# Sorting a recurrence's small matmuls by shape: within-chunk products first, state products after, and block scores in one written-out order

## The chip, the cores and the metric

The kernel runs on one core of one Trainium2 chip. The metric is the device time of one execution, in microseconds (us), lower is better. A core has a matmul engine (TensorE, PE in the profile; its weight loads are shown apart as PEld), three engines for vectors and scalars (VectorE or DVE, ScalarE or ACT, GpSimd or POOL) and a queue that issues most of the DMA transfers (SyncE or SP). Each engine works through its own list of instructions in order, and the engines wait for each other by semaphores.

## The reference, cut to what matters

One layer of a diffusion trunk over 640 tokens (128 of a prompt, 512 latent ones) of width 1024: an input projection, three groups of heads that read it (A: differential attention, B: a bidirectional gated linear recurrence, C: grouped-query attention), an output projection, and a squared-ReLU MLP. The change is in group B, which has four heads with a 64x64 state in each direction, scanned in chunks of 64 tokens:

```python
def step(S, xs):                       # one chunk of one direction
    qc, kc, vc, gc = xs
    b = jnp.cumsum(gc, axis=1)
    o_inter = jnp.einsum('bthk,bhkv->bthv', qc * jnp.exp(b), S)            # state product
    ...
    attn = jnp.einsum('bthk,bshk,btshk->bths', qc, kc, decay)              # scores in the chunk
    o_intra = jnp.einsum('bths,bshv->bthv', attn, vc)                      # within-chunk product
    S = jnp.exp(b_end)[..., None] * S + jnp.einsum('bshk,bshv->bhkv', kc * jnp.exp(b_end[:, None] - b), vc)
    return S, o_inter + o_intra
```

## The kernel before

Everything is float32. Large products (projections, MLP) split both operands in a high and a low part and take three matmuls for each product; these have a stationary operand of 128x128 and are called the GEMMs below. The small products of group B are plain float32 matmuls. The profile records each float32 matmul as two instructions, so that a count in the profile is twice the count in the program.

Group B works head by head (h = 0 to 3). Both directions are stacked on the 128 partitions, rows 0 to 63 forward and 64 to 127 backward. The 640 tokens are 10 chunks of 64, in 5 pairs of 128 tokens, and the pairs are taken in two groups, of 2 and 3 pairs.

- `b_scores(h)` makes the scores `att`, group by group. The score matrix of a chunk can't be made by one matmul, because the decay between two tokens is a ratio of exponentials that would overflow. It is built from levels: for L = 32, 16 and 8, VectorE and ScalarE write scaled keys and queries `lk[L]`, `lq[L]` (the tile `b_lqk`), and `blocks` multiplies them block by block. Level 32 has blocks of 64 and starts the accumulation in `pl`; level 16 has blocks of 32 and adds to `pl`; level 8 has blocks of 64 into `p8`. All these contract over 128 rows. Then come the two 64-row products of the tiles `k8` and `q8` (forward rows `F`, backward rows `R`) into the PSUM tile `ps2`, and the undecayed product of keys and queries into `pd`. `pl`, `p8` and `pd` lie in one PSUM tile, `pslv` in the profile; `ps2` is `psl`. ScalarE copies `pl` to `att`, and VectorE overwrites the entries that the four masks name from `p8`, from both halves of `ps2` and from `pd` (COPY_PREDICATED).
- `b_state(h)` makes the state updates (`psu`), VectorE scans them chunk by chunk into `st`.
- `b_out(h)` makes the output in the PSUM tile `psob`: for each of the 10 chunks the within-chunk product (64 rows of `att` with 64 rows of the values, rows and output partitions alternating between the halves) and then the state product (`qhat` with `st`, 128 rows), which adds to it.

A scheduler decides the order in each engine's list; it lets GEMMs and the adaLN products (`psada`) of other steps stand between the small matmuls. A `tc.manual_schedule` block keeps the matmuls in it in the order in which they are written, though other steps can still come between them. The calls at the end set the rough order: the scores of heads 0 to 3, the GEMMs `psgb` (gate) and `psA` (group A), and the adaLN columns lie around each other, then attention, output projection and MLP. PSUM tiles of the tag `s`, which `pslv`, `psl`, `psu` and `psob` share, have two buffers. Weights come through two raw buffers (`wr`) and are split by ScalarE and VectorE into five pairs of `wh` and `wl`, which the adaLN weights (`wad`) also use.

Of the kernel before, what the change touches and what calls it, by code (L numbers as in the profile page):

```python
# [28 lines left out]
HD = 64  # L29
# [13 lines left out]
CH = 64  # L43
NCH = NTOK // CH
# [19 lines left out]
def hybrid_layer_kernel(ctx: ExitStack, tc: tile.TileContext, T):  # L64
    nc = tc.nc
    V, A, G, PE = nc.vector, nc.scalar, nc.gpsimd, nc.tensor
# [96 lines left out]
    ib = mixed[:, 0:2, :].rearrange("p a (b c) -> p (a b c)", c=P).rearrange("p (t v) -> p t v", v=256)  # L163
# [6 lines left out]
    with ExitStack() as sctx:  # L170
# [66 lines left out]
        with tc.manual_schedule(engines={mybir.EngineType.PE}):  # L237
            for j in range(NK):
# [21 lines left out]
                r = sp.tile([P, 2 * P], F32, tag="adar", name=f"adar{j}", bufs=2)  # L260
# [26 lines left out]
    def ps_o(name):  # L287
        return pps.tile([P, 512], F32, tag="o", name=name, bufs=2)

    def ps_s(name):  # L290
        return pps.tile([P, 1024], F32, tag="s", name=name, bufs=2)

    def p1t(tag, shape, dtype=F32, bufs=1, name=None):
        return p1.tile(shape, dtype, tag=tag, name=name or tag, bufs=bufs)
# [134 lines left out]
    lq, lk = {}, {}  # L429
# [5 lines left out]
    def mrep(i, n):  # L435
        return masks[:, i : i + 1, :].to_broadcast([P, n, CH])

    F, R = slice(0, HD), slice(HD, P)
# [9 lines left out]
    def b_scores(h):  # L448
        k, b = bk[h], bb[h]
        hc = slice(h * HD, (h + 1) * HD)  # L450
        q = p1t(("a_kd0", "u6")[h % 2], [P, NTOK], name=f"b_q2{h}")
        src = bq[h // 2][(h % 2) * HD : (h % 2 + 1) * HD, :]
        A.copy(q[F], src)
        A.copy(q[R], src)
        att = p1t(("a_kd1", "u7")[h % 2], [P, NT, CH], name=f"b_att{h}")
        qhat = p1t(("a_kl", "u8")[h % 2], [P, NTOK], name=f"b_qh{h}")
        dec = p1t("b_dec", [P, NCH], bufs=2, name=f"b_dec{h}")
        st = sts[h % 2]
        stn = p1t("b_stn", [P, HD], bufs=2, name=f"b_stn{h}")
        nc.gpsimd.dma_start(st[F, 2, :], T["state_b_fwd"][h])  # L460
        nc.gpsimd.dma_start(st[R, NCH - 1, :], T["state_b_bwd"][h])
        bc = b.rearrange("p (c t) -> p c t", t=CH)
        A.activation(dec[F], bc[F, :, CH - 1], AF.Exp)
        A.activation(dec[R], bc[R, :, 0], AF.Exp)
        bend = p1t("b_end", [P, NCH], bufs=2, name=f"b_end{h}")
        V.tensor_copy(bend[F], bc[F, :, CH - 1])
        V.tensor_copy(bend[R], bc[R, :, 0])
        A.activation(qhat, b, AF.Exp)
        V.tensor_tensor(qhat, qhat, q, op=ALU.mult)
        khts = []  # L470
        for p0, npair in GROUPS:
            n = npair * P
            nch = 2 * npair
            t0 = p0 * P
            sl = slice(t0, t0 + n)
            av = att[:, p0 : p0 + npair, :]
            qv, kv, bv = q[:, sl], k[:, sl], b[:, sl]


            kq = p1t(("a_vl", "u9")[h % 2], [P, 2, GMAX], name=f"b_kq{h}{p0}")  # L480
            kh, q8 = kq[:, 0, :], kq[:, 1, :]
            for c in range(nch):
                cc = slice(c * CH, (c + 1) * CH)
                A.activation(kh[:, cc], bv[:, cc], AF.Exp, scale=-1.0, bias=bend[:, 2 * p0 + c : 2 * p0 + c + 1])
            V.tensor_tensor(kh[:, 0:n], kh[:, 0:n], kv, op=ALU.mult)
            pt = ps_o(f"pskht{h}{p0}")
            for c in range(npair):
                PE.transpose(pt[:, c * P : (c + 1) * P], kh[:, c * P : (c + 1) * P], ident)
            kht = p1t("b_kht", [P, GMAX], bufs=2, name=f"b_kht{h}{p0}")
            A.copy(kht[:, 0:n], pt[:, 0:n])  # L490
            khts.append(kht)


            def blocks(dst, kt, qt, w, first, rows_=slice(0, P)):
                for i in range(n // w):
                    o = i * w % P
                    tc_ = slice(i * w, (i + 1) * w)
                    c0 = i * w // P * CH + i * w % CH
                    PE.matmul(dst[o : o + w, c0 : c0 + w], kt[rows_, tc_], qt[rows_, tc_],  # L499
                              start=first, stop=True, skip_group_check=True)  # L500

            def vw(ps):
                return ps[:, 0 : npair * CH].rearrange("p (c t) -> p c t", t=CH)

            ps1 = ps_s(f"pslv{h}{p0}")
            pl, p8, pd = ps1[:, 0:512], ps1[:, 512:768], ps1[:, 768:1024]
            for L in LEVELS:
                dt = p1t("tmp", [P, GMAX], bufs=3, name=f"b_d{h}{p0}{L}")
                d3 = dt[:, 0:n].rearrange("p (m l) -> p m l", l=2 * L)
                b3 = bv.rearrange("p (m l) -> p m l", l=2 * L)  # L510
                V.tensor_tensor(d3, b3, b3[:, :, L : L + 1].to_broadcast([P, n // (2 * L), 2 * L]), op=ALU.subtract)
                A.activation(d3[:, :, 0:L], d3[:, :, 0:L], AF.Exp, scale=sgn[:, 0:1])
                A.activation(d3[:, :, L : 2 * L], d3[:, :, L : 2 * L], AF.Exp, scale=sgn[:, 1:2])
                for r, src, dst, lo in ((F, k, lk[L], 0), (F, q, lq[L], L), (R, q, lq[L], 0), (R, k, lk[L], L)):
                    V.tensor_tensor(
                        dst[r, 0:n].rearrange("p (m l) -> p m l", l=2 * L)[:, :, lo : lo + L],
                        src[r, sl].rearrange("p (m l) -> p m l", l=2 * L)[:, :, lo : lo + L],
                        d3[r, :, lo : lo + L], op=ALU.mult)
                if L == 8:
                    blocks(p8, lk[L], lq[L], CH, True)  # L520
                else:
                    blocks(pl, lk[L], lq[L], 2 * L, L == 32)
            A.copy(av, vw(pl))
            V.copy_predicated(av, mrep(0, npair), vw(p8))

            d8 = p1t("tmp", [P, GMAX], bufs=3, name=f"b_d8{h}{p0}")
            k8 = p1t("tmp", [P, GMAX], bufs=3, name=f"b_k8{h}{p0}")
            d3 = d8[:, 0:n].rearrange("p (m l) -> p m l", l=8)
            b3 = bv.rearrange("p (m l) -> p m l", l=8)
            V.tensor_tensor(d3, b3, b3[:, :, 4:5].to_broadcast([P, n // 8, 8]), op=ALU.subtract)  # L530
            A.activation(q8[:, 0:n], d8[:, 0:n], AF.Exp)
            A.activation(k8[:, 0:n], d8[:, 0:n], AF.Exp, scale=-1.0)
            V.tensor_tensor(q8[:, 0:n], q8[:, 0:n], qv, op=ALU.mult)
            V.tensor_tensor(k8[:, 0:n], k8[:, 0:n], kv, op=ALU.mult)
            ps2 = ps_s(f"psl8{h}{p0}")
            blocks(ps2[:, 0:512], k8, q8, CH, True, F)
            blocks(ps2[:, 512:1024], k8, q8, CH, True, R)
            blocks(pd, kv, qv, CH, True)
            V.copy_predicated(av, mrep(1, npair), vw(ps2[:, 0:512]))
            V.copy_predicated(av, mrep(2, npair), vw(ps2[:, 512:1024]))  # L540
            V.copy_predicated(av, mrep(3, npair), vw(pd))

        return hc, att, qhat, dec, st, stn, khts
# [28 lines left out]
    def b_out(h, parts):  # L572
        hc, att, qhat, dec, st, stn, khts = parts
        po = ps_s(f"psob{h}").rearrange("p (e c) -> p e c", e=2)
        for c in range(NCH):
            e, pr = c % 2, c // 2
            r = slice(e * CH, (e + 1) * CH)
            d = po[r, e, pr * HD : (pr + 1) * HD]
            PE.matmul(d, att[r, pr, :], ib[r, pr, hc], start=True, stop=False)
            PE.matmul(d, qhat[:, c * CH : (c + 1) * CH], st[:, c, :], start=False, stop=True)  # L580
        for e in range(2):
            r = slice(e * CH, (e + 1) * CH)
            A.copy(ob[r, :, hc], po[r, e, 0 : NT * HD].rearrange("p (t v) -> p t v", v=HD))
# [404 lines left out]
    def scores(h):  # L988
        parts[h] = b_scores(h)
# [65 lines left out]
    ada(2, "a_q0")  # L1055
    tok["gb"](2)
    b_out(0, parts[0])
    tok["gb"](4)
    b_state(1, parts[1])
    gates(3)  # L1060
    tok["gb"](0)
    tok["gb"](3)
    tok["gb"](1)
    b_out(1, parts[1])
    ada(7, "a_q1")
    scores(2)
# [14 lines left out]
    lam_()  # L1081
    gr[0].tiles[4]()
    b_out(2, parts[2])
    prep(0)
    prep_ctx(0)
# [319 lines left out]
```

## Time and profile before

| | |
|---|---|
| median of 3 runs | 977.85 us (974.32 to 980.61) |
| the profiled execution | 977.37 us, span 975.6 us |
| mean granted TensorE clock over the span | 0.976 |
| PE busy / DVE busy / ACT busy | 940.7 / 574.2 / 432.9 us |
| group B's small products lie between | 72 and 232 us of the span |

A row of the timeline has the start of the first instruction, the time from there to the end of the last, the engine, the line, the operation with output and inputs, the shape of the stationary operand (rows*columns), the moving operand, and how many instructions are merged; in brackets stands how long the engine was idle before, and what ended it. Matmuls overlap in the pipeline, so the step from one start to the next is the pace, not the duration. A row of the windows has the stretch in us, its length, the busy time of PE with its instruction count, the granted clock (1.00 is full speed), and the share and rate of DMA.

### The profile page before, as it was taken

The numbers are of one execution on the slowest core, as the hardware profiler recorded it, in microseconds if no ns is written. First come the engines' busy times: TensorE is split into PE (matmuls) and PEld (weight loads), VectorE is DVE, ScalarE is ACT, GpSimd is POOL, SyncE is SP. The second block draws the span as 40 slices with busy tenths as digits, with TensorE's granted clock in tenths as the row PEclk, the third lists the DMA queues.
The fourth block names the chain that finished last, engine by engine and source line by source line (L and its number), as shares of the span: only waits on it lengthen the run. The fifth ranks groups of instructions, "written<-read, shape, count | busy, mean of one in ns | idle before, by whom it ended". The sixth has DMA issues, their size and how long they took to land.

```text
span 975.6 us, 15543 instructions
## 1 busy us (share of the span) xinstructions
PE 940.7 (96%) x6133; PEld 811.0 (83%) x6133; DVE 574.2 (59%) x1123; ACT 432.9 (44%) x916; POOL 53.6 (5%) x108
## 2 busy tenths in 40 slices
PE   6989999999999998899999999999999999999996
PEld 4878787789998887677889999999998888888885
DVE  2378976876878788884586322333335434473448
ACT  3576654444756566754286222232224334143320
POOL 2200010121000110001000000000000000000000
PEclk9998988989999999999999999999999999999998
DMA  9942512621303212014203322523312121052102
GB/s 260 286 143 66 172 50 68 180 57 50 92 18 102 89 48 64 24 65 151 76 22 98 109 68 84 173 90 106 87 65 87 65 87 66 29 166 87 65 15 93
DMA packets 95753, 90.82 MB, mean 93 GB/s; under 512 B 5793, under 2 KB 81281, under 8 KB 95681
## 3 DMA queue, kind: packets, MB, share of 16 engines
q1 hardware_dynamic: 91936, 82.50, 28.0%
q0 software_dynamic: 3552, 7.27, 2.7%
q8 instruction: 48, 0.79, 0.3%
q14 instruction: 25, 0.20, 0.1%
q10 hardware_dynamic: 192, 0.08, 0.0%
HBM read 86.41 MB, written 3.41 MB: 92 GB/s over the span
## 4 chain that ended last, share of the span: by engine, by line
PE 86%; DVE 6%; ACT 3%; DMA 2%; SPq 1%; issue 1%; DVEq 0%; ACTq 0%
PE psy L130 8%; PE psf L1267 8%; PE psf L1268 8%; PE psf L1269 8%; PE psy L129 8%; PE psy L128 8%; PE psA L128 3%; PE psA L129 3%; PE psA L130 3%; PE psavA L726 2%; PE pswo L130 2%; PE pswo L129 2%; PE pswo L128 2%; PE psavC L948 2%; PE pslv L499 1%; PE pstA L716 1%
## 5 line engine op out<-in xcount | busy, mean ns | idle before, releaser
L1267 PE MATMUL psf<-xh,wf_h 128*128 128x320 f32 x512 | 158.7, 310 | 0.0
L1268 PE MATMUL psf<-xl,wf_h 128*128 128x320 f32 x512 | 158.1, 309 | 0.0
L1269 PE MATMUL psf<-xh,wf_l 128*128 128x320 f32 x512 | 158.1, 309 | 0.0
L130 PE MATMUL psy<-wg_h,xl 128*128 128x512 f32 x320 | 127.7, 399 | 0.0
L129 PE MATMUL psy<-wg_l,xh 128*128 128x512 f32 x320 | 126.1, 394 | 0.0
L128 PE MATMUL psy<-wg_h,xh 128*128 128x512 f32 x320 | 125.5, 392 | 0.0
L91 DVE TENSOR_TENSOR xl<-hid,xh 128x640 fp32r<-128x640 f32 x64 | 52.1, 824 | 85.9 <-ACT xh L90 85.9
L90 ACT CAST xh<-hid 128x640 fp32r<-128x640 f32 x64 | 45.6, 727 | 121.1 <-PE psy L129 115.6
L1267 PEld LDWEIGHTS psf<-xh,wf_h 128*128 128x128 f32 x512 | 96.3, 188 | 1.7 <-issue 1.2
L1268 PEld LDWEIGHTS psf<-xl,wf_h 128*128 128x128 f32 x512 | 96.3, 188 | 0.0
L1269 PEld LDWEIGHTS psf<-xh,wf_l 128*128 128x128 f32 x512 | 96.3, 188 | 0.0
L1272 DVE TENSOR_TENSOR hid<-hid,psf 128x320 f32<-128x320 f32 x64 | 31.1, 485 | 106.7 <-ACT hid L1271 106.7
L1271 ACT ACTIVATE hid<-psf 128x320 f32<-128x320 f32 x64 | 28.0, 438 | 120.2 <-PE psf L1269 120.2
L129 PEld LDWEIGHTS psy<-wg_l,xh 128*128 128x128 f32 x320 | 60.1, 188 | 15.7
L128 PEld LDWEIGHTS psy<-wg_h,xh 128*128 128x128 f32 x320 | 60.1, 188 | 14.1
L130 PEld LDWEIGHTS psy<-wg_h,xl 128*128 128x128 f32 x320 | 60.1, 188 | 13.9
L91 DVE TENSOR_TENSOR wf_l<-wf_r,wf_h 128x1024 fp32r<-128x1024 f32 x32 | 39.2, 1224 | 37.8 <-ACT wf_h L90 37.8
L128 PE MATMUL psA<-wa_h,xh 128*128 128x384 f32 x160 | 57.1, 359 | 0.0
L129 PE MATMUL psA<-wa_l,xh 128*128 128x384 f32 x160 | 56.4, 352 | 0.0
L130 PE MATMUL psA<-wa_h,xl 128*128 128x384 f32 x160 | 56.1, 350 | 0.0
L90 ACT CAST wf_h<-wf_r 128x1024 fp32r<-128x1024 f32 x32 | 33.7, 1054 | 32.9 <-PE psf L1268 27.6
L91 DVE TENSOR_TENSOR wg_l<-wg_r,wg_h 128x1024 fp32r<-128x1024 f32 x32 | 39.2, 1224 | 7.5 <-ACT wg_h L90 4.9
(475 smaller groups left out, 1946.6 us busy)
## 6 DMA issues: line engine op xcount, KB each, us to landing
wad<-in_w_ada SPq DMA_DIRECT2D x32, 512.0 KB, 4.6
wf_r<-in_w_ff SPq DMA_DIRECT2D x32, 512.0 KB, 4.1
wg_r<-in_w_ff SPq DMA_DIRECT2D x32, 512.0 KB, 3.6
adaw<-in_w_ada SPq DMA_DIRECT2D x32, 256.0 KB, 5.2
wa_r<-in_w_in SPq DMA_DIRECT2D x48, 128.0 KB, 2.6
wo_r<-in_w_out SPq DMA_DIRECT2D x8, 512.0 KB, 3.7
x<-in_x_sample SPq DMA_DIRECT2D x8, 256.0 KB, 4.8
wc_r<-in_w_in SPq DMA_DIRECT2D x4, 512.0 KB, 3.7
```

Source lines behind the costliest of these rows:

```text
L90: A.copy(hi, src)
L91: V.tensor_tensor(lo, src, f32(hi), op=ALU.subtract)
L128: PE.matmul(ps, s[0], m[0], start=start, stop=False)
L129: PE.matmul(ps, s[0], m[1], start=False, stop=False)
L130: PE.matmul(ps, s[1], m[0], start=False, stop=stop)
L726: PE.matmul(po, pT[:, c, :], vals(g, c, c0, n), start=(c == 0), stop=(c == NKC - 1))
L948: PE.matmul(g.po[r, n * P : (n + 1) * P], v, w[:, c, :], start=(c == 0), stop=(c == NKC - 1))
L1267: PE.matmul(ps[:, 0:HALF], h, xh[:, k, sl], start=(k == 0), stop=False)
L1268: PE.matmul(ps[:, 0:HALF], h, xl[:, k, sl], start=False, stop=False)
L1269: PE.matmul(ps[:, 0:HALF], l, xh[:, k, sl], start=False, stop=(k == NK - 1))
L1271: A.activation(hs, ps[:, 0:HALF], AF.Relu)
L1272: V.tensor_tensor(hs, hs, ps[:, 0:HALF], op=ALU.mult)
```

## The change

In `b_scores` the calls of `blocks` leave the loop over the levels. All of a group's block scores now stand in one written-out sequence behind the products of VectorE that feed them, sorted by the shape of the block: level 32, level 8 and the undecayed product (128 rows, 64 columns), level 16 (128 rows, 32 columns), then the two products of 64 rows. The copies to `att` follow behind all of them. In `b_out` all ten within-chunk products come first and then all ten state products; the accumulation is started once for each half, by chunks 0 and 1.

```diff
                         d3[r, :, lo : lo + L], op=ALU.mult)
-                if L == 8:
-                    blocks(p8, lk[L], lq[L], CH, True)
-                else:
-                    blocks(pl, lk[L], lq[L], 2 * L, L == 32)
-            A.copy(av, vw(pl))
-            V.copy_predicated(av, mrep(0, npair), vw(p8))
...
             ps2 = ps_s(f"psl8{h}{p0}")
-            blocks(ps2[:, 0:512], k8, q8, CH, True, F)
-            blocks(ps2[:, 512:1024], k8, q8, CH, True, R)
-            blocks(pd, kv, qv, CH, True)
+            with tc.manual_schedule(engines={mybir.EngineType.PE}):
+                blocks(pl, lk[32], lq[32], 64, True)
+                blocks(p8, lk[8], lq[8], CH, True)
+                blocks(pd, kv, qv, CH, True)
+                blocks(pl, lk[16], lq[16], 32, False)
+                blocks(ps2[:, 0:512], k8, q8, CH, True, F)
+                blocks(ps2[:, 512:1024], k8, q8, CH, True, R)
+            A.copy(av, vw(pl))
+            V.copy_predicated(av, mrep(0, npair), vw(p8))
             V.copy_predicated(av, mrep(1, npair), vw(ps2[:, 0:512]))
...
         po = ps_s(f"psob{h}").rearrange("p (e c) -> p e c", e=2)
-        for c in range(NCH):
-            e, pr = c % 2, c // 2
-            r = slice(e * CH, (e + 1) * CH)
-            d = po[r, e, pr * HD : (pr + 1) * HD]
-            PE.matmul(d, att[r, pr, :], ib[r, pr, hc], start=True, stop=False)
-            PE.matmul(d, qhat[:, c * CH : (c + 1) * CH], st[:, c, :], start=False, stop=True)
+        def d(c):
+            return po[c % 2 * CH : (c % 2 + 1) * CH, c % 2, c // 2 * HD : (c // 2 + 1) * HD]
+
+        with tc.manual_schedule(engines={mybir.EngineType.PE}):
+            for c in range(NCH):
+                r = slice(c % 2 * CH, (c % 2 + 1) * CH)
+                PE.matmul(d(c), att[r, c // 2, :], ib[r, c // 2, hc], start=c < 2, stop=False, skip_group_check=True)
+            for c in range(NCH):
+                PE.matmul(d(c), qhat[:, c * CH : (c + 1) * CH], st[:, c, :], start=False, stop=c >= NCH - 2,
+                          skip_group_check=True)
```

The instructions are the same ones in the same number on every engine. What the scheduler makes of the new order differs from before only up to the start of attention; POOL's list is unchanged, and in SP's list a weight load of group A moves ahead of adaLN loads once.

The first place is `b_out(0)` on PE, between GEMMs of the gate (`psgb`). Before:

```order
L129 MATMUL psgb4_1553<-wgb_l1_1421,xh_69 128x256
L130 MATMUL psgb4_1553<-wgb_h1_1422,xl_70 128x256
L579 MATMUL psob0_1530<-mixed_83,b_att0_733 64x64
L580 MATMUL psob0_1530<-b_st0_663,b_qh0_734 64x64
L579 MATMUL psob0_1530<-mixed_83,b_att0_733 64x64
L580 MATMUL psob0_1530<-b_st0_663,b_qh0_734 64x64
```

and now:

```order
L129 MATMUL psgb4_1568<-wgb_l1_1433,xh_69 128x256
L581 MATMUL psob0_1542<-mixed_83,b_att0_733 64x64 x10
L583 MATMUL psob0_1542<-b_st0_663,b_qh0_734 64x64 x10
L130 MATMUL psgb4_1568<-wgb_h1_1434,xl_70 128x256
L553 MATMUL psu1_1594<-mixed_83,b_kht10_1258 128x64 x4
```

The two kinds alternated ten times (the first two of the ten pairs are shown); now ten of one kind are followed by ten of the other.

The second place is the second group of head 2 on PE, whose first rows wait for VectorE's `b_lqk32` and whose transposes `pskht22` wait for VectorE's `b_kq22`. Before:

```order
L499 MATMUL psl820_1817<-b_kq20_1756,b_k820_1811 64x64 x8
L143 MATMUL psada4608_1928<-wad4608_0_1929,cs_71 32x256 x4
L143 MATMUL psada4608_1928<-wad4608_1_1931,cs_71 32x256
L499 MATMUL pslv20_1767<-b_q22_1740,mixed_83 64x64 x4
L143 MATMUL psada4608_1928<-wad4608_1_1931,cs_71 32x256 x3
L143 MATMUL psada4096_1947<-wad4096_0_1948,cs_71 32x256
L499 MATMUL pslv22_1847<-b_lqk32_657 64x64 x6
```

and now, carried on to the end of the group's scores (the rows left out are adaLN products and GEMMs of `psA00`):

```order
L499 MATMUL psl820_1817<-b_kq20_1774,b_k820_1811 64x64 x8
L143 MATMUL psada4608_1952<-wad4608_0_1953,cs_71 32x256 x4
L143 MATMUL psada4608_1952<-wad4608_1_1955,cs_71 32x256 x4
L143 MATMUL psada4096_1971<-wad4096_0_1972,cs_71 32x256 x4
L143 MATMUL psada4096_1971<-wad4096_1_1974,cs_71 32x256
L499 MATMUL pslv22_1868<-b_lqk32_657 64x64 x6
...
L488 MATMUL pskht22_1862<-ident_62,b_kq22_1854 128x128 x3
...
L129 MATMUL psA00_2021<-wa0_l2_2006,xh_69 128x384
L499 MATMUL pslv22_1868<-b_lqk8_661 64x64 x6
L499 MATMUL pslv22_1868<-b_q22_1758,mixed_83 64x64 x6
L499 MATMUL pslv22_1868<-b_lqk16_659 32x32 x12
L499 MATMUL psl822_1900<-b_kq22_1854,b_k822_1894 64x64 x12
```

The undecayed product of the group ahead has left the middle of the adaLN products, and level 8, the undecayed product, level 16 and the 64-row products of this group now stand in one run.

The third place is VectorE's list at the same point, from the last operand of `psl820` to the first operand of `pslv22`. Before:

```order
L485 TENSOR_TENSOR b_kq30_2171<-b_kq30_2171,b_k3_1610 128x256
L91 TENSOR_TENSOR wa0_l0_1966<-wa0_r0_1965,wa0_h0_1967 128x768
L533 TENSOR_TENSOR b_kq20_1756<-b_kq20_1756,b_q22_1740 128x256
L534 TENSOR_TENSOR b_k820_1811<-b_k820_1811,mixed_83 128x256
L511 TENSOR_TENSOR b_d2232_1848<-mixed_83 128x384
L511 TENSOR_TENSOR b_d2216_1862<-mixed_83 128x384
L91 TENSOR_TENSOR wa0_l1_1974<-wa0_r1_1973,wa0_h1_1975 128x768
L515 TENSOR_TENSOR b_lqk32_657<-mixed_83,b_d2232_1848 64x6x32
```

and now:

```order
L527 TENSOR_TENSOR b_kq20_1774<-b_kq20_1774,b_q22_1758 128x256
L528 TENSOR_TENSOR b_k820_1811<-b_k820_1811,mixed_83 128x256
L511 TENSOR_TENSOR b_d2232_1869<-mixed_83 128x384
L511 TENSOR_TENSOR b_d2216_1877<-mixed_83 128x384
L91 TENSOR_TENSOR wa0_l0_1990<-wa0_r0_1989,wa0_h0_1991 128x768
L91 TENSOR_TENSOR wa0_l1_1998<-wa0_r1_1997,wa0_h1_1999 128x768
L515 TENSOR_TENSOR b_lqk32_657<-mixed_83,b_d2232_1869 64x6x32
```

Both splits of group A's weights (`wa0_l0`, `wa0_l1`) now stand between the operands of `psl820` and those of `pslv22`, where one stood before.

## The prediction

> **What bounds the kernel now.** The page comes first. PE is busy nearly all the time, and the chain that ended last runs over PE for 86% of the span:
>
> ```profile
> PE 940.7 (96%) x6133; PEld 811.0 (83%) x6133; DVE 574.2 (59%) x1123; ACT 432.9 (44%) x916; POOL 53.6 (5%) x108
> PE 86%; DVE 6%; ACT 3%; DMA 2%; SPq 1%; issue 1%; DVEq 0%; ACTq 0%
> ```
>
> So a microsecond taken out of PE's list is worth about a microsecond, as long as PE finds its operands ready. But "busy" doesn't mean at full pace. The windows of the four `b_out` calls, one row for each head, show how long they are:
>
> ```profile
> 128.14:133.28 5.14, 5.14 (x42) 1.00 0.01 3
> 147.30:153.60 6.30, 6.30 (x41) 0.75 0.45 128
> 207.09:212.44 5.35, 5.35 (x42) 0.94 0.16 45
> 226.68:231.81 5.13, 5.13 (x41) 1.00 0.01 3
> ```
>
> Each is 40 small instructions, and together they take 21.92 us. The timeline of PE at the first one shows why they are slow:
>
> ```profile
> 127.81 0.28 PE L129 MATMUL psgb<-wgb_l,xh 128*128 128x256 f32 x1
> 127.93 0.28 PE L130 MATMUL psgb<-wgb_h,xl 128*128 128x256 f32 x1
> 128.14 0.33 PE L579 MATMUL psob<-mixed,b_att 64*64 64x64 f32 x2
> 128.40 0.33 PE L580 MATMUL psob<-b_st,b_qh 128*64 128x64 f32 x2
> ...
> 133.02 0.33 PE L580 MATMUL psob<-b_st,b_qh 128*64 128x64 f32 x2
> 133.28 0.56 PE L128 MATMUL psgb<-wgb_h,xh 128*128 128x256 f32 x1
> 133.64 0.41 PE L129 MATMUL psgb<-wgb_l,xh 128*128 128x256 f32 x1
> 133.85 0.41 PE L130 MATMUL psgb<-wgb_h,xl 128*128 128x256 f32 x1
> ```
>
> A step from a 64*64 product to a 128*64 product takes 0.26 us for two instructions. The GEMMs ahead, four times as wide, step by 0.12 us. Behind `b_out` the same GEMMs step by 0.21 us: the clock has been halved.
>
> Where the same shapes stand in a row, they are several times faster:
>
> ```profile
> 87.96 0.57 PE L499 MATMUL pslv<-b_q,b_k 128*64 128x64 f32 x12
> 88.46 0.41 PE L129 MATMUL psfb<-xl,wfb_h 128*128 128x320 f32 x1
> ...
> 89.10 0.74 PE L499 MATMUL psl<-b_kq,b_k 64*64 64x64 f32 x24
> 89.77 0.41 PE L129 MATMUL psfb<-xl,wfb_h 128*128 128x320 f32 x1
> ...
> 102.14 1.33 PE L553 MATMUL psu<-mixed,b_kht 64*128 64x64 f32 x20
> 103.40 0.44 PE L488 MATMUL pskht<-ident,b_kq 128*128 128x128 f32 x2
> ```
>
> Twelve 128*64 instructions take 0.50 us up to the next start, 24 of 64*64 take 0.67 us, both with the change to the next shape in them. A GEMM's step of 0.12 us becomes 0.21 where the small shape follows (127.93 to 128.14). So the change of shape costs, not the small product; and `psu`, which alternates the two halves of the rows at one shape, steps by 1.26/20 = 0.06 us, so alternating halves is not what costs.
>
> The windows along the clock show the second loss:
>
> ```profile
> 133.33:140.15 6.82, 6.82 (x41) 0.50 0.15 43
> 153.60:157.22 3.62, 3.62 (x44) 0.50 0.01 5
> 212.44:218.66 6.22, 5.67 (x22) 0.50 0.34 93
> 232.32:235.73 3.41, 3.41 (x15) 0.50 0.31 77
> 160.60:164.00 3.40, 3.40 (x62) 1.00 0.13 24
> 109.43:112.85 3.42, 1.18 (x14) 1.00 0.04 9
> 112.85:116.26 3.41, 3.41 (x27) 0.50 0.05 10
> ```
>
> All four `b_out` calls run into or are followed by half clock. The last two rows show the same behind a stretch in which PE was busy for only 1.18 of 3.42 us. A stretch with 62 small instructions densely packed (160.60 on) is not followed by it. I read from this that an alternating `b_out` counts as too little work for the clock, and a dense one might not.
>
> **The change part by part.** The sum is made against the profiled execution, 977.37 us (span 975.6 us, 1.8 around it); the median shown, 977.85, is within 0.5 us of it.
>
> *A, the sorted `b_out`.* Twenty 64*64 instructions at 0.67/24 are 0.56 us, twenty 128*64 at 0.50/12 are 0.83 us; each rate holds one change of shape, as the new list has: 1.4 us a head. Gain 21.92 - 4 x 1.4 = 16.3 us.
>
> *B, the clock behind it.* Beyond the `b_out` rows themselves the half clock covers 6.82 + 3.62 + 5.67 (busy part) + 3.41 = 19.5 us of PE. At full clock the step falls from 0.21 to 0.12, by 43%: 8.4 us. It is bounded by 0 (the clock falls all the same) and 8.4. I take three of four, 6.3 us, since the stretch behind head 1 gets waits of its own (D).
>
> *C, the block scores.* The five blocks of a group (levels 32, 16, 8, undecayed, the 64-row pair) stood mostly alone among GEMMs and adaLN products. The list now has mostly three runs: level 32; then 8, undecayed and 16; then the 64-row pair. So this is not one sequence in PE's list, only a tighter one. A block alone pays about 0.1 us to enter (0.21 - 0.12) and about as much to leave; two of five go and one change within a run comes: 0.2 to 0.3 us a group, 8 groups, 0 to 2.6 us. Three groups had three blocks in a row before, and in the stage of heads 0 and 1 VectorE has hardly any idle time to give (third busy column of this row of the windows of all engines: 9.77 of 10 us), so I take 1.5 us.
>
> ```profile
> 110.00:120.00 10.00, 8.01 (x68) 6.19 (x68) 9.77 (x23) 5.28 (x16) 1.50 (x2) 0.83 0.19 62
> ```
>
> *D, new waits.* This is where the gain can get lost. Behind head 1's `b_out` PE was late and VectorE waited for it:
>
> ```profile
> 148.05 0.41 DVE L534 TENSOR_TENSOR b_k<-b_k,mixed 128x256 f32<-128x256 f32 x1
> 148.38 1.02 DVE L511 TENSOR_TENSOR b_d<-mixed 128x384 f32<-128x384 f32 x2
> 149.32 0.95 DVE L91 TENSOR_TENSOR wa_l<-wa_r,wa_h 128x768 fp32r<-128x768 f32 x1
> 156.90 0.35 DVE L515 TENSOR_TENSOR b_lqk<-mixed,b_d 64x192 f32<-64x192 f32 x1 [6.64 <-PE pslv L499]
> 159.62 0.30 DVE L539 COPY_PREDICATED b_att<-masks,psl 128x128 f32<-128x128 uint8 x1
> 160.75 0.54 DVE L485 TENSOR_TENSOR b_kq<-b_kq,mixed 128x384 f32<-128x384 f32 x1
> 158.31 0.47 PE L499 MATMUL psl<-b_kq,b_k 64*64 64x64 f32 x16
> ```
>
> The operand of `psl820` was done at 148.46 and PE came at 158.31, 9.85 us later. By then PE gains two `b_out` calls (5.14 + 6.30 - 2.8 = 8.6), the half clock behind them (10.4 x 0.43 = 4.5) and about 1 us before: 14. VectorE gains only what it waited for PE; its scan of head 1's states follows `psu1`, so I put that at 4 to 5 us. The 9.85 us of cover are then used up, and both arrive together. From there to `pskht22`, VectorE's new list holds two differences (1.0), two weight splits (1.9), four products of level 32 (1.4), one pair of columns (0.35), four masked copies (1.2), four products of level 16 (1.4) and the key product (0.54): 7.8 us. PE has 16 instructions of `psl820`, 32 of adaLN products, 12 of level 32 and 4 of columns, 64 in all, an estimated 3.5 us from the row at 160.60 (62 in 3.40 us). So PE waits about 4 us, in front of `pslv22` and `pskht22`. Queued behind these waits on PE stand the tile 0 of `psA` and all that follows. Another 0.5 us goes before `psl822`, which needs VectorE's last products. I take -4.5 us, between 0 (VectorE has more lead) and -8 (head 3, which has the same order with a GEMM of 24 steps as cover, waits as well).
>
> The longest wait of head 1 stays:
>
> ```profile
> 111.99 0.45 PE L499 MATMUL pslv<-b_q,b_k 128*64 128x64 f32 x8 [2.24 <-DVE b_att L524]
> ```
>
> It goes with the undecayed product's old place behind a masked copy, but the 64-row pair now comes first there, and its operand is made by the same busy VectorE at nearly the same time. I count 0. In SP's list the moved weight load had been ready before the adaLN loads that it now passes; 0 too. From attention on the lists are the same, and PE's time before it moves everything forward.
>
> Sum: 16.3 + 6.3 + 1.5 - 4.5 = 19.6 us, so 977.4 - 19.6 = **957.8 us**.
>
> **The Trainium skill** speaks against A at one place. Its page "TensorE: Matmul & The Clock Gate", Part 3, says that a weight load overlaps matmuls in flight only when its row group differs. State products use all 128 rows each, so sorted they would load one after the other:
>
> ```profile
> L580 PEld LDWEIGHTS psob<-b_st,b_qh x80: 132/136/227, 128.4 to 231.6; 128*64 128x64 f32 x80
> ```
>
> By the rule a head's 20 loads would cost 20 x 0.136 = 2.7 us, not 0.83. The twelve 128*64 instructions above took 0.50 us with loads of the same size, 0.04 each, so the trace disagrees. The same page of the Trainium skill, Part 1, says that the clock falls after a window of idle PE of about 3.4 us. By that rule `b_out` would not be the cause, since PE's records fill it, and B would not come.
>
> **The rivals.**
>
> 1. *The clock falls all the same* (B is 0): small dense work of 1.4 us inside GEMMs may still be too little, or the waits of D halve the clock. For it: row 109.43, where waiting did that. Against it: row 160.60. 977.4 - (16.3 + 1.5 - 4.5) = 964.1 us.
> 2. *VectorE takes the place of PE* further on: D is -8 at heads 2 and 3, and the clock falls in these waits, so that B is 0 and C 0.5: 977.4 - (16.3 + 0.5 - 8) = 968.6 us. For it: the 7.8 us of VectorE against 3.5 of PE in D. Against it: VectorE waited for PE in the row at 156.90, for 6.64 us.
> 3. *Loads in series* in the state products: A falls by 4 x 1.9 = 7.6, which makes 965.4 us.
> 4. *Slower*: the runs hold PE in order at every group. Level 8 heads a run, and behind it wait the undecayed product and level 16, which are ready or cheap, and all GEMMs. If each of the 8 groups waits as long as PE did at its worst place, 3.1 us for `b_kq` (row below), and gets 3.41 us of half clock behind it (1.5 us lost), this is 37 us against gains of 24: 990 us. It decides from about 3 us of wait and lost clock at every group. Against it: that row is the first of the whole recurrence, with no earlier head's work to cover it, and level 32 is still followed by GEMMs that cover the wait for level 8.
>
> ```profile
> 71.50 0.44 PE L488 MATMUL pskht<-ident,b_kq 128*128 128x128 f32 x2 [3.09 <-DVE b_kq L485]
> ```
>
> **How the numbers follow.** About 1% (9.8 us) is what a measurement can tell from no change. The forecast (950 to 962) has 0.64, the clock rival 0.13, VectorE 0.10, loads in series 0.05, slower 0.04, and 0.04 stays for better than 948. The best bound is 16.3 + 8.4 + 2.6 - 0 = 27.3, 950 us, with 2 us more if the wait at 111.99 shrinks too; the worst of the likely cases is 969. Range 948 to 969. Faster by over 1% (below 967.6) takes the forecast, the better case, clock, loads and a fifth of VectorE: 0.88. Slower by over 1% has 0.03 of rival 4's 0.04, and within 1% the rest, 0.09.
>
> **What would show it.** A: `psob` as 20 + 20 instructions in about 1.4 us a head. B: granted clock 1.00 in the 7 us behind heads 0, 2 and 3. C: group B's GEMMs with fewer long steps. D: idle PE in front of `pslv` and `pskht` of head 2's second group, released by `b_lqk` and `b_kq`. The prediction is wrong if a sorted `b_out` still takes over 2.5 us, if half clock follows it, or if PE waits for VectorE by more than 8 us in all between 128 and 232.

## The result, and the profile after

The changed kernel takes 951.84 us (median of 4 runs, 950.49 to 953.69) where the kernel before, run beside it, takes 977.92 (974.32 to 980.61): ratio 0.9737, 95% interval 0.9699 to 0.9774. The forecast was 957.8 in a range of 948 to 969. The profiled execution takes 952.96 us, 24.4 less than the one of before; all sums below are made between these two. Line numbers are those of the changed kernel: `b_out` is now L581 (within-chunk) and L583 (state), the block scores are still L499, the adaLN column products are L976.

The page after, busy times and the shares of the chain that ended last:

```profile
PE 912.9 (96%) x6133; PEld 792.2 (83%) x6133; DVE 573.6 (60%) x1123; ACT 432.7 (45%) x916; POOL 53.5 (6%) x108
PE 80%; DVE 11%; ACT 3%; DMA 3%; issue 1%; SPq 1%; DVEq 0%; ACTq 0%
```

PE's busy time fell by 27.8 us (940.7 to 912.9) with the same 6133 instructions, and its idle time in the span rose from 34.9 to 38.3 us, by 3.4. So 27.8 came in and 3.4 went back. VectorE's share of the chain rose from 6 to 11%.

The first `b_out` in PE's timeline (start, us, engine, line, operation, count):

```profile
127.17 0.28 PE L129 MATMUL psgb<-wgb_l,xh 128*128 128x256 f32 x1
127.37 0.80 PE L581 MATMUL psob<-mixed,b_att 64*64 64x64 f32 x20
128.10 0.80 PE L583 MATMUL psob<-b_st,b_qh 128*64 128x64 f32 x20
128.83 0.39 PE L130 MATMUL psgb<-wgb_h,xl 128*128 128x256 f32 x1
```

It runs from 127.37 to 128.83, 1.46 us instead of 5.14, and the next GEMM isn't stretched. The windows of PE, for this call, the stretch behind it, the one behind head 1's call up to 144.98, the one that follows, and those behind the calls of heads 2 and 3 (length, PE busy, granted clock, DMA share, GB/s):

```profile
127.37:128.83 1.46, 1.46 (x41) 1.00 0.00 0
128.83:135.60 6.77, 6.77 (x68) 1.00 0.15 46
140.70:144.98 4.28, 2.05 (x37) 1.00 0.02 8
145.99:149.40 3.41, 3.41 (x58) 0.50 0.66 182
193.85:199.00 5.15, 4.19 (x31) 1.00 0.30 81
208.73:214.00 5.27, 5.27 (x35) 1.00 0.16 50
```

No `b_out` is followed by half clock any more. The one half-clock stretch left between 116 and 361 us stands behind a stretch in which PE was busy for only 2.05 of 4.28 us. Without the last 8 us of the span, the clock's record has 41.0 us at half before and 20.5 us now.

The block scores of head 1's second group. Before, each block stood alone among GEMMs:

```profile
124.59 0.28 PE L130 MATMUL psgb<-wgb_h,xl 128*128 128x256 f32 x1
124.80 0.74 PE L499 MATMUL psl<-b_kq,b_k 64*64 64x64 f32 x24
125.47 0.38 PE L128 MATMUL psgb<-wgb_h,xh 128*128 128x256 f32 x1
125.70 0.28 PE L129 MATMUL psgb<-wgb_l,xh 128*128 128x256 f32 x1
```

and now level 8, undecayed, level 16 and the 64-row pair stand in one run:

```profile
122.94 0.57 PE L499 MATMUL pslv<-b_lqk 128*64 128x64 f32 x12
123.34 0.52 PE L499 MATMUL pslv<-b_q,b_k 128*64 128x64 f32 x12
123.79 0.40 PE L499 MATMUL pslv<-b_lqk 128*32 128x32 f32 x24
124.12 0.74 PE L499 MATMUL psl<-b_kq,b_k 64*64 64x64 f32 x24
124.79 0.39 PE L128 MATMUL psgb<-wgb_h,xh 128*128 128x256 f32 x1
```

A block alone costs 0.09 us in front (124.59 to 124.80 is 0.21, where a GEMM's step is 0.12) and 0.11 behind (125.47 to 125.70). It also costs 0.05 to 0.1 inside where it is 128*64: 0.40 and 0.45 us for twelve in the run, 0.50 alone in the row at 87.96 of the prediction. Counted over the whole trace, block scores stand in 18 places instead of 33. Together with the step of the instruction ahead of each, at full clock and without waits, they take 20.6 us instead of 25.0.

The waits. The longest new one, in the list of PE's waits between 100 and 230 us and in PE's timeline, and ScalarE's timeline ahead of it:

```profile
PE psada L976 <- ACT ada L145: 2.2, 1, 2.2
PE psadag L143 <- DMA wad<-in_w_ada: 1.4, 1, 1.4
```
```profile
144.98 0.61 PE L976 MATMUL psada<-selc,ada 128*128 128x2 f32 x4 [2.23 <-ACT ada L145]
```
```profile
139.75 0.40 ACT L512 ACTIVATE b_d<-b_d,sgn 128x128 f32<-128x128 f32 x1 [1.91 <-DVE b_d L511]
...
140.96 0.82 ACT L90 CAST wa_h<-wa_r 128x768 fp32r<-128x768 f32 x1
...
144.55 0.37 ACT L145 COPY ada<-psada 128x256 f32<-128x256 f32 x1
```

PE reaches the column products of adaLN part 7 before ScalarE has copied their operand. ScalarE is late because it waited for VectorE's `b_d` until 139.75 and then had eleven operations, counted from that one, in front of the copy. The wait of head 1's first group is still there, 2.4 us for `b_k`.

### The profile page after: what moved, and what is told of

Read it like the earlier page. It is cut to its first block, busy times and chain, and to the rows that moved or that the text cites. A ratio compares the mean times of both kernels' runs of the same rounds, so it can differ in the third digit from the quotient of the medians.

```text
span 951.2 us, 15540 instructions
## 1 busy us (share of the span) xinstructions
PE 912.9 (96%) x6133; PEld 792.2 (83%) x6133; DVE 573.6 (60%) x1123; ACT 432.7 (45%) x916; POOL 53.5 (6%) x108
## 3 DMA queue, kind: packets, MB, share of 16 engines
HBM read 86.41 MB, written 3.41 MB: 94 GB/s over the span
## 4 chain that ended last, share of the span: by engine, by line
PE 80%; DVE 11%; ACT 3%; DMA 3%; issue 1%; SPq 1%; DVEq 0%; ACTq 0%
PE psf L1271 8%; PE psy L130 8%; PE psf L1272 8%; PE psf L1273 8%; PE psy L129 8%; PE psy L128 8%; PE psA L129 2%; PE psA L130 2%; PE psavA L730 2%; PE psA L128 2%; PE pswo L130 2%; PE pswo L129 2%; PE pswo L128 2%; DVE b_st L560 2%; PE psavC L952 2%
```

## The experiments

Each kernel ran beside the kernel before, whose median there was 975.5 to 978.3 us. Ratios are against it.

**1. The sorted `b_out` alone.** The kernel before with the new `b_out` and the old order of the scores.

> The kernel before with the sorted b_out alone; the block scores stay in their old order. My theory: nearly all of the gain of 26 us is the sorted b_out (16 us in the four calls themselves, 8 us in the clock behind them), and the scores' new order is worth its 1.5 us less what it loses in new waits. So 952 to 955 us, psob in 1.4 to 1.5 us a head, granted clock 1.00 in the 7 us behind heads 0 and 3. Rival (the scores carry part of it, because the shape changes in them were under-priced): 957 to 961 us.

Measured: 957.94 us, ratio 0.9793 (0.9755 to 0.9831), 20.0 us less. `psob` takes 1.46 us a head and half clock follows none of the four calls, but the time lies in the rival's range: `b_out` carries 20 of the 26 us, not nearly all. The wait at the adaLN columns comes with the sorted `b_out` alone: PE waits 1.58 us there, is busy for 1.95 of the 3.41 us around it (147.97 to 151.38), and the next 10.2 us are at half clock. In all, the profiled execution, the slowest of the six with 962.25 us, has 37.6 us at half, where the changed kernel has 20.5: half clock has left `b_out` and stands behind waits of PE instead, which took back part of the gain in that execution.

**2. The scores alone.** The changed kernel with the old `b_out`.

> The changed kernel with the old alternating b_out; only the block scores are in the new order. My theory: PE is as late as before, so the new waits are covered and only the 0 to 2.6 us of saved shape changes show: 975 to 978 us, with the half clock behind every b_out as before. Rival (the scores carry part of the gain): 970 to 973 us. Second rival (the runs hold PE in order and cost by themselves): 980 us or more.

Measured: 973.98 us, ratio 0.9945 (0.9917 to 0.9974), 4.0 us less by the medians, where the interval allows 2.5 to 8.1: more than my theory, and close to the 4.4 us counted above. With experiment 1, 24.0 of the 26.1 us are the sum of the two parts; the rest is within the noise. In this kernel half clock stands behind heads 0, 1 and 3, but not behind head 2, although PE alternates there as long as anywhere:

```profile
201.48:206.60 5.12, 5.12 (x41) 1.00 0.07 16
206.60:213.00 6.40, 5.88 (x38) 1.00 0.41 115
```

So an alternating `b_out` mostly, not always, brings the clock down.

**3. Alternating with a lag.** Does the change of shape cost, or the accumulation onto the block just written?

```
-for c: within-chunk(c)
-for c: state(c)
+for i in range(NCH + 6):
+    if i < NCH: within-chunk(i)
+    if i >= 6:  state(i - 6)
```

> The changed kernel with b_out in an order that alternates again, but with a lag: six within-chunk products, then 14 pairs (within-chunk product of chunk i, state product of chunk i - 6), then six state products; so a product never adds to the block that the one just before it wrote. About 28 changes of shape a head instead of 1, with none of the back-to-back accumulation. My theory (the change of shape costs about 0.1 us, (5.14 - 1.46) / 38): 1.46 + 27 x 0.097 = 4.1 us a head, so 952 + 10.5 = 962 us, and up to 970 if half clock follows. Rival (the cost was the state product's wait for the block that the within-chunk product had just written): 1.5 us a head and 952 us.

My count was wrong: a head has ten chunks, and each product is two instructions in the trace. So only four pairs alternate, with 7 changes of shape, not 28. PE's timeline:

```profile
127.93 0.68 PE L582 MATMUL psob<-mixed,b_att 64*64 64x64 f32 x14
128.54 0.33 PE L585 MATMUL psob<-b_st,b_qh 128*64 128x64 f32 x2
128.80 0.33 PE L582 MATMUL psob<-mixed,b_att 64*64 64x64 f32 x2
...
130.08 0.68 PE L585 MATMUL psob<-b_st,b_qh 128*64 128x64 f32 x14
130.69 0.39 PE L130 MATMUL psgb<-wgb_h,xl 128*128 128x256 f32 x1
```

A step in the middle is 0.26 us, just as in the old list, though no product adds to the block that the last one wrote. A head takes 2.76 us, 1.30 more than sorted for 6 more changes: 0.22 us each. This holds also what a product loses that has no neighbour of its own size beside it (experiment 6). The clock stays at full speed behind it. The whole takes 953.03 us (ratio 0.9733, 0.9683 to 0.9782): of 5.2 us more in PE's list 1.2 shows, because PE now comes later to the wait at 144.98, and that wait is gone.

**4. The sorted list four times.** Does 5.8 us of small products bring the clock down?

```
+for rep in range(4):
     for c: within-chunk(c)
     for c: state(c)
```

> The changed kernel with b_out's sorted sequence issued four times (20 + 20 products, four times over; each repeat starts the sums anew): 160 small products densely packed, about 4 x 1.46 = 5.8 us a head, longer than the alternating list was (5.14 us). My theory (the clock falls behind changes of shape, not behind small products): full clock behind it, 4 x 4.4 = 17.5 us more than the changed kernel, 969 us or a little less where PE had been waiting anyway. Rival (any 5 us of small products halves the clock, and the sorted list escapes only because it is short): half clock behind heads 0, 2 and 3 again, 8 us more, 976 to 978 us.

Measured: 972.01 us, ratio 0.9935 (0.991 to 0.9961), 20.2 us more than the changed kernel. The windows of heads 0 and 2, and what follows each:

```profile
126.55:132.39 5.84, 5.84 (x161) 1.00 0.06 18
132.39:139.00 6.61, 6.61 (x67) 1.00 0.09 33
203.07:208.91 5.84, 5.84 (x162) 1.00 0.12 34
208.91:215.00 6.09, 6.08 (x38) 1.00 0.48 131
```

160 small instructions in 5.84 us, longer than the alternating 40 in 5.14, and the clock stays at 1.00, as it does behind heads 1 and 3. So it isn't the length of the small work. The whole is 2.7 us above the 17.5 forecast; PE's idle time in the profiled execution is 43.8 us, 5.5 more.

**5. One size, alternating.** The within-chunk product reads all 128 rows, so it also sums the other chunk of the pair, which the layer leaves out.

```
-PE.matmul(d(c), att[r, c // 2, :], ib[r, c // 2, hc], ...)
+PE.matmul(d(c), att[:, c // 2, :], ib[:, c // 2, hc], ...)   # and state(c) right behind it
```

> The changed kernel with b_out strictly alternating again (within-chunk product, state product, chunk after chunk, each state product adding to the block just written), but the within-chunk product reads all 128 rows, as the state product does, so that all 20 products of a head have one size. It sums both chunks of a pair where one was meant; the number of instructions is the same. My theory (a change of the tile's size costs 0.2 us, and neither the alternation nor the accumulation does): 40 instructions of 128*64 at 0.73/20 are 1.46 us a head, full clock behind them, 950 to 955 us. Rival (two products that add to one block one behind the other wait for each other): 5.1 us a head as before, half clock behind it, 972 to 976 us.

```profile
127.76 0.34 PE L580 MATMUL psob<-mixed,b_att 128*64 128x64 f32 x4
127.93 0.29 PE L581 MATMUL psob<-b_st,b_qh 128*64 128x64 f32 x4
...
129.12 0.39 PE L130 MATMUL psgb<-wgb_h,xl 128*128 128x256 f32 x1
```

A head takes 1.36 us (127.76 to 129.12), strictly alternating and adding to the block just written. The whole takes 953.64 us (ratio 0.975, 0.9712 to 0.9788). With experiment 3 this settles what was asked: the change of the tile's size costs, and neither the alternation nor the accumulation onto the block just written does.

**6. Sorted, but half by half.** Even chunks first, then odd ones, in each run.

> The changed kernel with b_out sorted by shape as well, but within each run the even chunks come first and then the odd ones: neighbours use the same half of the array instead of alternating halves. My theory as predicted (only the number of shape changes counts): 1.5 us a head and 952 us. Rival (a run of one shape is fast because neighbours in different halves run side by side): a product no longer overlaps its neighbour, about 0.11 us each as for psu, so 10 x 0.11 x 2 = 2.2 to 2.5 us a head, 4 us more, 955 to 957 us.

```profile
126.27 1.20 PE L582 MATMUL psob<-mixed,b_att 64*64 64x64 f32 x20
127.40 1.20 PE L584 MATMUL psob<-b_st,b_qh 128*64 128x64 f32 x20
128.53 0.38 PE L130 MATMUL psgb<-wgb_h,xl 128*128 128x256 f32 x1
```

2.26 us a head instead of 1.46: the rival is right about `b_out`. A run of one size is fast also because neighbours in different halves of the array run side by side. My reading "shape alone" holds for 2.9 of the 3.7 us saved a head (5.14 - 2.26), which is 0.16 us for each of the 18 changes saved; the other 0.8 is this. The whole takes 952.70 us (ratio 0.9739, 0.97 to 0.9777). Of the 3.2 us more in the four calls, nothing shows. The wait for ScalarE's copy shrinks from 2.23 to 0.95, but one of 1.3 for `b_kq` comes, and PE's idle time is 39.5 us instead of 38.3. What makes up for it is the clock: no half clock follows that wait, and the record has 10.2 us at half instead of 20.5, worth 4.4 us at 0.43.

The page "TensorEngine Tiling (Array Packing)" of the Trainium skill, Tiling Modes, says both: that a change of the tiling mode drains the engine, and that tiles of one mode work independently. The trace agrees with a price of the change, 0.22 us in experiment 3, without showing the drain itself, and with the second, 1.46 us against 2.26 here.

**7 and 8. The adaLN product of part 7 earlier, and later.** One statement moves ahead of `b_out(1)`, or behind `scores(2)`.

```
+ada(7, "a_q1")          # 7
 b_out(1, parts[1])
-ada(7, "a_q1")
 scores(2)
+ada(7, "a_q1")          # 8
```

> The changed kernel with one statement moved: the adaLN product of part 7 stands ahead of head 1's b_out instead of behind it, so that ScalarE can copy its rows while PE works on b_out, and its column products stand inside b_out's list. My theory: the wait of 2.23 us for that copy (at 144.98) and the half clock behind it (3.41 us) were the price of PE being early; both go: 948 to 950 us. Rival (PE then waits as long at the next operand of VectorE): 952 us, with a wait of about 2 us in front of pskht or pslv of head 2. Third possibility: the copy isn't done in time and PE waits inside b_out: 953 to 955 us.

> The changed kernel with the adaLN product of part 7 moved the other way: behind the scores of head 2. My theory: the wait for ScalarE's copy of its rows goes, but the adaLN products no longer cover VectorE's work for the group, so PE waits there for b_lqk or b_k instead, as the prediction's step D had it: 951 to 953 us with 2 to 4 us of waits on VectorE in head 2. Rival (VectorE has lead enough): 948 to 949 us.

Measured: 952.95 us (ratio 0.9742, 0.971 to 0.9774) and 953.51 us (0.9747, 0.9713 to 0.9782); 1.1 and 1.7 us above the changed kernel, whose own runs spread over 3.2 us, so no difference shows. Earlier, PE meets the same wait of 2.1 us in the middle of `b_out(1)`, as the third possibility had it. Later, PE waits 0.8 us there and otherwise behind VectorE's splits and key product, as my theory had it, though the time lies above its 951 to 953 us:

```profile
PE psl L499 <- DVE wa_l L91: 1.6, 1, 1.6
PE pskht L488 <- DVE b_kq L485: 1.3, 1, 1.3
```

In both, the wait belongs to the stage, not to the instruction that shows it.

**9 and 10. The splits of attention head 0's weights on GpSimd:** the casts (9), or the subtractions (10).

```
-A.copy(hi, raw); V.tensor_tensor(lo, raw, hi, subtract)
+G.tensor_copy(hi, raw); V.tensor_tensor(lo, raw, hi, subtract)   # 9
+A.copy(hi, raw); G.tensor_tensor(lo, raw, hi, subtract)          # 10
```

> The changed kernel; the casts of attention head 0's weights (4 of 128x768, 0.82 us each on ScalarE, two of them between 140.9 and 142.8 in front of the copy that PE waits for) go to GpSimd, which is idle there. My theory: PE's waits in head 2 are now set by two full engines, ScalarE for the adaLN rows and VectorE for the rest. With ScalarE relieved by 1.6 us the wait of 2.23 us falls to about 0.6, and VectorE's operands come next: 950 to 951 us. Rival (ScalarE alone is what holds PE): all of the 2.2 us and the 3.41 us of half clock behind it go, 948 us. Third possibility: GpSimd's cast is slow or disturbs VectorE, and psA or the subtractions start late: 953 us or more.

> The changed kernel; the subtractions that split attention head 0's weights (4 of 128x768, 0.91 to 0.95 us each on VectorE, two of them at 143.16) go to GpSimd. My theory: the wait for ScalarE's copy at 144.98 stays near 2.2 us, since ScalarE's list is untouched, and VectorE's lead behind it grows: 951 to 952 us, no difference to be measured. Rival (VectorE, as the prediction's step D had it, sets the end of this stage): 2 to 4 us less, 948 to 950 us. Third possibility: GpSimd's subtraction takes well over 2 us each and psA, which needs all four, starts late: 954 us or more.

Measured: 964.15 us (ratio 0.9866, 0.9831 to 0.9901) and 963.17 us (0.9855, 0.9826 to 0.9884), both some 12 us slower than the changed kernel: the third possibility. VectorE's operations stop beside GpSimd's. The timelines of the two engines, of experiment 9 and then of experiment 10:

```profile
137.04 0.28 DVE L519 TENSOR_TENSOR b_lqk<-b_q,b_d 64x128 f32<-64x128 f32 x1
...
137.33 0.84 POOL L122 CAST wa_h<-wa_r 128x768 fp32r<-128x768 f32 x1
137.33 1.31 DVE L519 TENSOR_TENSOR b_lqk<-mixed,b_d 64x128 f32<-64x128 f32 x2
```
```profile
141.76 4.13 POOL L123 TENSOR_TENSOR wa_l<-wa_r,wa_h 128x768 fp32r<-128x768 f32 x2 [3.96 <-ACT wa_h L122]
142.06 4.24 DVE L515 TENSOR_TENSOR b_d<-mixed 128x384 f32<-128x384 f32 x2
```

Beside a cast of 0.84 us two products take 1.31 us that take 0.28 each alone. Beside two subtractions (2.05 to 2.40 us each on GpSimd, 0.94 to 0.96 on VectorE) the two differences `b_d` take 4.24 us, 1.02 in the changed kernel. ScalarE, which needs `b_d`, then comes still later to the copy that PE waits for: 3.4 us in experiment 9, although ScalarE had been relieved of the casts, and 4.1 us in 10. So a lighter ScalarE doesn't shorten that wait; that VectorE sets it, through ScalarE's list, is what the two runs point to, but the order of ScalarE's list changed as well. In the profiled executions PE's idle time is 47.7 us in experiment 9 and 51.5 in 10, against 38.3 in the changed kernel, with PE's busy time 2 to 3 us lower, so the loss stands in PE's waits. Part of it lies where both edits reorder the lists up to attention, some 3 us at `pscs`; why PE waits there stays open.

**11. More changes of size in a group's sequence.** Level 16 and the undecayed product are cut in two and interleaved.

```
-blocks(pd, ...); blocks(pl, level 16, ...)
+for hf in range(2):
+    blocks(pl, level 16, ..., half=hf); blocks(pd, ..., half=hf)
```

> The changed kernel; in each group's sequence level 16 (128*32) and the undecayed product (128*64) are each cut in two and interleaved: half of 16, half of undecayed, half of 16, half of undecayed. The same instructions, two more changes of tile size in each of the 8 groups, 16 in all. It asks why the scores were worth 4 us where I had forecast 1.5. My theory (each block that stood alone cost 0.3 us to enter and leave, more than the 0.2 that I took; a single change within the sequence is 0.15 us, as in b_out's list, (5.14 - 2.26) / 18): 16 x 0.15 = 2.4 us more of PE time, of which head 2's groups hide some: 953 to 955 us. Rival (changes between block scores are nearly free, and the scores' gain came from their place in the list): 952 us, and a group's sequence as long as before, 1.85 us for 48 + 24 instructions in front of 124.79.

```profile
123.97 0.82 PE L500 MATMUL pslv<-b_lqk 128*64 128x64 f32 x24
124.72 0.45 PE L500 MATMUL pslv<-b_q,b_k 128*64 128x64 f32 x6
125.09 0.32 PE L500 MATMUL pslv<-b_lqk 128*32 128x32 f32 x12
125.34 0.45 PE L500 MATMUL pslv<-b_q,b_k 128*64 128x64 f32 x6
125.71 0.74 PE L500 MATMUL psl<-b_kq,b_k 64*64 64x64 f32 x24
126.39 0.39 PE L128 MATMUL psgb<-wgb_h,xh 128*128 128x256 f32 x1
```

The first row merges level 8 with the first half of level 16. The same 72 instructions take 2.42 us instead of 1.85 (122.94 to 124.79), 0.57 more. I had counted two more changes of size. There are three in this group, because level 8 and the undecayed product, which are of one size and stood side by side, are now apart: 8, 16, undecayed, 16, undecayed, 64-row pair has five changes, where the changed kernel has two. So a change costs 0.19 us, a little more than the 0.15 that I took. The whole takes 954.79 us (ratio 0.9768, 0.9729 to 0.9807), 2.95 more, where 0.57 in each of eight groups would make 4.6; in the profiled executions PE's busy time rises by 3.9 (912.9 to 916.8).

**12. Level 32 inside the sequence.**

```
-blocks(pl, level 32); blocks(p8, level 8); blocks(pd, undecayed); ...
+blocks(p8, level 8); blocks(pd, undecayed); blocks(pl, level 32); ...
```

> The changed kernel with level 32 moved inside a group's sequence: level 8, undecayed, level 32, level 16, 64-row pair. In PE's list level 32 then stands next to the others in every group and no longer by itself; the block scores stand in 12 places instead of 18. My theory (a block that stands by itself costs about 0.3 us to enter and leave, as the scores alone showed): 6 x 0.3 = 1.8 us less, 950 us. Rival (level 32 by itself gave PE something to do while VectorE made level 8, so its time turns into waits in head 2): 952 to 954 us.

Measured: 958.8 us, the median of five executions from 954.3 to 962.2 us (a sixth took 1756 us); ratio 0.9803 (0.9764 to 0.9842), 7 us slower than the changed kernel. Its waits between 60 and 230 us:

```profile
PE pskht L488 <- DVE b_kq L485: 6.4, 4, 3.1
PE psl L499 <- DVE b_stn L560: 2.4, 2, 1.8
PE pslv L499 <- DVE b_lqk L515: 1.8, 1, 1.8
```

The scores' own steps fall by 2.0 us, as my theory says (20.6 to 18.6), but PE now waits for VectorE at many places, as the rival says and by more: its idle time is 44.7 us instead of 38.3. That is rival 4 of the prediction, not reached in the changed kernel because level 32 stays loose there. None of these versions beats the changed kernel.

## Why the prediction was right

By its own steps, between the two profiled executions: gain 24.4 us, forecast 19.6.

- **A**, forecast 16.3, measured 21.92 - 4 x 1.46 = 16.1. The sum was right, in part by luck: the two runs of a head take 0.73 us each, where the rates read from `psl` and `pslv` gave 0.56 and 0.83, and the two misses nearly cancel. The reason was incomplete: the change of size is 2.9 us a head, neighbours side by side 0.8 (experiments 3, 5, 6). Rival 3 is out: ten state products take 0.73 us for 20 instructions with a load of 0.138 us each.
- **B**, forecast 6.3 of 8.4, measured 7.2 to 7.3. The half clock is 20.5 us shorter; 3.8 of that lay inside `b_out` and is in A, and 16.7 x 0.43 = 7.2. PE's 27.8 less 16.1 and 4.4 leave 7.3. Rival 1 (clock falls all the same) is out by the windows of after and by experiment 4. The reason that I gave for three of four, new waits behind head 1, came true: the one stretch of half clock left there follows the new wait.
- **C**, forecast 1.5 with a bound of 2.6, measured 4.4 in PE's steps and 4.0 as a kernel of its own. This is the term that was mis-sized. The number of places that go was right (15 of 33, two a group). The price was not: I took 0.2 us for a place and gave 0.1 back for the change inside, where a lone block costs 0.2 at its ends and up to 0.1 inside, 4.4 / 15 = 0.29 net. The discount for VectorE's lack of idle time isn't borne out either: experiment 2 has the whole gain.
- **D**, forecast -4.5, measured -3.4 in PE's idle time. The size and the head were right, the place and the path were not, so the size is in part luck. PE waits at the adaLN columns, 2.23 us, within the first group of head 2, and not in front of `pslv22` and `pskht22` in the second; the scheduler had set those columns inside the run ahead. I had compared VectorE's list with PE's and left out ScalarE, which stands between the two. The cover was not used up either: the operand of `psl820` is done at 142.31 and PE comes to it at 146.38, 4.1 us later, because VectorE gained 6.2 us (148.46 to 142.31) where I took 4 to 5, and PE was held by the wait above. Experiment 8 shows that the wait moves to VectorE's operands when those columns move behind the scores. A DMA wait of 1.4 us at `psadag` also came, where 0.8 had been.
- The wait at 111.99 stayed, with another releaser, as said: 2.24 before, 2.43 now, for `b_k`.

The sum of the misses, -0.2 in A, +1.0 in B, +2.9 in C and +1.1 in D, is the 4.8 us by which the gain was larger.

## What to carry to other kernels

Read the step from start to start of small products by the shape of the neighbour: where a product steps by 0.26 us alternating and 0.07 in a run of its own size, sort by size, and within a size let neighbours use different halves of the array. Then look what VectorE and ScalarE owe the same stage, because a run made too strict turns the saved time into waits (experiment 12), and moving the instruction that waits doesn't help (7, 8). An idle GpSimd isn't free help for a full VectorE: measure it beside the work that it runs next to.

## What the runs showed of the hardware that I had not expected

- The clock falls to half while PE's records are full, if they alternate in size for about 5 us (four of four calls before, three of four in experiment 2), and not behind 5.84 us of dense small products. Nearly all half-clock stretches last 3.41 us or a multiple. Part 1 of the Trainium skill's page "TensorE: Matmul & The Clock Gate" gives a window of that length, and the trace agrees; that it needs an idle window doesn't fit these rows, unless the drains within an alternating list count as idle, which no run here settles. No run separates the changes of size from how few products fill a microsecond (40 instructions in 5.14 us against 160 in 5.84). Why one such call in eight went without is open too.
- The same page of the Trainium skill, Part 3, has loads overlap matmuls in flight only where the row group differs. The trace disagrees: sorted 128-row loads of 0.138 us stepped by 0.037 us a product instruction, and by 0.057 in one half of the array (experiment 6).
- VectorE all but stood still beside GpSimd: two differences of 128x384 took 4.24 us instead of 1.02 while GpSimd's two subtractions took 4.13 (experiment 10). The Trainium skill's page "Trainium Architecture — The Big Picture", section "What this means for kernel authors", calls the port that the two share an exclusive lock and not a split of bandwidth; the trace agrees.
